# A four-layer mixer trunk on one core: first weights ahead of the second modulation blocks, products after each chunk pair, two-pass gate products, a shorter reciprocal root, and another order in the last pair's halves

## The chip, the core and the metric

The kernel runs on one core of a Trainium2 chip. TensorE (PE) multiplies matrices, VectorE (DVE), ScalarE (ACT) and GpSimd (POOL) work on elements, SyncE (SP) and the queues of the other engines issue transfers. The metric is the time of one execution in device microseconds; lower is better. The figure that counts is the median of the runs of a kernel.

## The reference, cut to what matters

The trunk runs 512 latent tokens and 256 context tokens of width 1024 through four layers. Layer i uses mixer i % 3: a gated linear attention in chunks (GLA, layers 0 and 3), a windowed attention (layer 1), a recurrent unit (RG-LRU, layer 2). Each mixer is wrapped in norms with a modulation (shift, scale, gate) that comes from a conditioning vector. Only the latent tokens are returned.

```
def rmsnorm(x, g):
    xf = x.astype(jnp.float32)
    y = xf * lax.rsqrt(jnp.mean(xf * xf, axis=-1, keepdims=True) + EPS)
    return (y * g.astype(jnp.float32)).astype(x.dtype)
...
    def project(h):
        q, k, v, z = jnp.split(h @ w_in, [GLA_DK, 2 * GLA_DK, 2 * GLA_DK + GLA_DV], axis=-1)
        la_f, la_b = [split_heads(jax.nn.log_sigmoid(((h @ w_g1[d]) @ w_g2[d] + b_g[d]).astype(jnp.float32)) / GLA_TAU, GLA_HEADS)
                      for d in range(2)]
```

The change touches the gates' two small products (h @ w_g1 of rank 16 for each of two directions, then @ w_g2), the norms, and the order in which the first layer starts.

## The kernel before

**Tiling.** The width of 1024 is KC = 8 chunks of 128 rows. Activations lie transposed, 128 channels x 768 tokens for each chunk (256 context tokens, then 512 latent ones). Every operand of a large product is split in two terms of reduced precision, a high part and a remainder: `Rh` and `Rl` for activations, `wh` and `wl` for weights. One product is then three matmuls for each chunk (Rh with wh, Rl with wh, Rh with wl). Weights arrive as fp32 in a buffer `raw` (or `rawp` in the start); ScalarE casts the high part (L266) and VectorE, or GpSimd for every third, subtracts the remainder (L269).

**Stages.** `first_norm` reads x, normalises it, transposes it into `OG` and modulates it; then come the four mixers (`gla`, attention, LRU, `gla`), each followed by `finish`: out-projection (L796), post-norm, residual, and the next layer's norm and transposes (L638). A mixer's engines are ordered by a scheduler that goes by priorities. Two places have their order written out for TensorE, ScalarE and VectorE with `tc.manual_schedule`: the loop over n in `first_norm`, and the middle of `finish`.

**The start.** The modulation of layer 0 comes in eight blocks m of one MB. `mod_part` fetches a block (L511) and multiplies it with the conditioning vector (L524, into 32 partitions); `mod_ss` copies the result (L537), transposes it (L542) and adds it up to the scale and shift of two chunks (L543, L549, L555). Blocks n and n + 4 together give the modulation of chunks 2n and 2n + 1. `modulate` (L703, L704, L708) then makes Rh and Rl of a chunk. Round n of the loop takes blocks n and n + 4 and modulates two chunks. `products` (L728) are matmuls of the layer's first products, chunk by chunk as Rh and Rl appear: `todo[:2]` is the gates' first weight w1 (128 columns, of which each group of 32 holds the two directions' 16), `todo[2:]` the first head's q and k (`wqk`: k for the context, k and q for the latent tokens). The fetches are issued in the order x, blocks 0 and 4, w1 (`load_g1`), wqk, blocks 1 and 5, 2 and 6, 3 and 7, save that each `fetch` stands where the code puts it: the first one (w1) before blocks 1 and 5, the second (wqk) before blocks 3 and 7.

**The first head.** `gates` multiplies t1 (what w1 gave) with the second weight g2 (L979), applies log-sigmoid on ScalarE (L983 to L996) and builds running sums on VectorE (L989, L993). `levels` makes factors X and Y for each level of the chunked recurrence (L1049, L1110), copies Y to K (L1096) and multiplies them in small matmuls of 32 columns (L1062). `values` (L1034) are the head's v products. `spread` deals the side work (values) out between the levels, by a total in ns.

**The norms.** `rstd_of` turns a sum of squares into a reciprocal root with two GpSimd instructions: times 1/n plus EPS (L614), then a power of -0.5 (L615). It serves the norm of x (tile `rx`, 24 of them), the post-norm (`ry`, 22, after a reduction of two half sums in `post`, L810), and the gate-head norm (`ro`, 20).

**finish.** `halves(...)` runs the second 512 output columns for pairs of (half of the depth, tile of 128 tokens). After the second half of a tile it takes the square sums (L803) and the gate multiply (L804), and `post` makes the reciprocal root. `residual` (L816), `square` (L621) and `scale` (L823) follow, then the transposes of the pair.

## Time and profile before

| what | value |
|---|---|
| median of 3 runs | 1518.22 us (1516.42 to 1520.79) |
| profiled execution, its own time | 1513.64 us |
| its span in the profile | 1511.8 us |
| TensorE busy | 1442.0 us, 95% |
| VectorE, ScalarE, GpSimd busy | 67%, 52%, 13% |
| chain that ended last, by engine | PE 54%, DVE 10%, ACT 5%, DMA 4% |

The profiled execution is one run, and its time lies under the median of the three; durations of instructions are read from it. Stages in us from the span's start: start 0 to 62, layer 0 to 370, its finish to 455, layer 1 to 790, its finish to 880, layer 2 to 1115, its finish to 1226, layer 3 to 1460, its finish to the end. In a timeline row the first number is the start, the second the time that the named instructions took, and the bracket holds the idle time before them and what ended it.

### The profile page before, as it was taken

The page shows a single profiled execution, that of the slowest core. Times are in us where ns is not written, and L with a number is a line of the kernel's source. Part 1 is how long each engine was busy: PE and PEld are TensorE (multiplying, and loading weights), DVE is VectorE, ACT ScalarE, POOL GpSimd, SP SyncE. Part 2 cuts the span into 40 slices and gives each one's busy share as a digit, 9 for nine tenths or more (in the row PEclk, how much of TensorE's full clock was granted, in tenths as well). Part 3 has the DMA queues.
Part 4 walks back from the last instruction along what each step waited for, and adds up shares of the span by engine and source line. Part 5 has one row for each costly group of instructions (what it writes and reads, how often), then busy time and mean ns, then how long its engine had stood idle before and what let it go on. Part 6 is the DMA issues. An engine that isn't in the chain of part 4 may idle for free.

```text
span 1511.8 us, 29077 instructions
## 1 busy us (share of the span) xinstructions
PE 1442.0 (95%) x11691; PEld 1206.4 (80%) x11691; DVE 1010.5 (67%) x1914; ACT 784.2 (52%) x1541; POOL 189.4 (13%) x300
## 2 busy tenths in 40 slices
PE   5988999999999899999999999899999999999998
PEld 3877888888877778878888787788878778889886
DVE  5576657576264389787883568988972667676854
ACT  5535353624252367656662477878842555364441
POOL 2202100112022200010000210000011211101111
PEclk8999999999999999999999999999999999999999
DMA  9441514112574542122216625212252342121232
GB/s 300 145 147 53 169 38 135 57 34 76 203 237 140 174 112 68 31 65 57 57 56 224 217 79 152 82 50 71 67 177 64 103 145 91 46 60 57 60 111 85
DMA packets 153046, 162.35 MB, mean 107 GB/s; under 512 B 12418, under 2 KB 141968, under 8 KB 152912
## 3 DMA queue, kind: packets, MB, share of 16 engines
q1 hardware_dynamic: 147456, 146.56, 31.4%
q10 hardware_dynamic: 5456, 13.94, 2.6%
q8 instruction: 92, 1.51, 0.4%
q14 instruction: 42, 0.34, 0.1%
HBM read 138.44 MB, written 11.53 MB: 99 GB/s over the span
## 4 chain that ended last, share of the span: by engine, by line
PE 54%; DVE 10%; ACT 5%; DMA 4%; issue 2%; SPq 1%; POOL 1%; ACTq 0%; DVEq 0%; POOLq 0%
PE mxt L796 14%; PE pjt L395 9%; PE pjt L385 9%; PE pjt L1034 4%; PE mxt L1532 3%; PE mxt L1516 2%; PE sct L1637 2%; PE mxt L524 1%; PE mxt L1475 1%; PE mxt L1194 1%; DVE wl L269 1%; PE mxt L1458 1%; DMA bb<-in_b_mod_dram 1%; DMA raw<-in_w_mod_dram 1%; PE sct L1062 1%
## 5 line engine op out<-in xcount | busy, mean ns | idle before, releaser
L385 PE MATMUL pjt<-Rh,wh 128*128 128x256 f32 (+1 forms) x592 | 199.0, 337 | 5.3 <-DVE Rh L649 3.3
L385 PE MATMUL pjt<-Rl,wh 128*128 128x256 f32 (+1 forms) x592 | 198.2, 336 | 2.0 <-DVE Rl L650 1.6
L385 PE MATMUL pjt<-Rh,wl 128*128 128x256 f32 (+1 forms) x592 | 197.1, 334 | 0.7 <-DVE wl L269 0.7
L269 DVE TENSOR_TENSOR wl<-raw,wh 128x1024 fp32r<-128x1024 f32 x106 | 129.7, 1237 | 51.2 <-ACT wh L266 50.6
L395 PE MATMUL pjt<-Rh,wl 128*128 128x512 f32 (+1 forms) x448 | 160.3, 358 | 0.0
L395 PE MATMUL pjt<-Rl,wh 128*128 128x512 f32 (+1 forms) x448 | 159.8, 357 | 0.0
L395 PE MATMUL pjt<-Rh,wh 128*128 128x512 f32 (+1 forms) x448 | 159.5, 356 | 0.0
L266 ACT CAST wh<-raw 128x1024 fp32r<-128x1024 f32 x118 | 121.4, 1051 | 71.6 <-PE mxt L796 33.0
L796 PE MATMUL mxt<-wh,Rh 128*128 128x512 f32 x352 | 138.9, 395 | 0.0
L796 PE MATMUL mxt<-wh,Rl 128*128 128x512 f32 x352 | 137.6, 391 | 0.8 <-DVE Rl L769 0.8
L796 PE MATMUL mxt<-wl,Rh 128*128 128x512 f32 x352 | 137.2, 390 | 0.0
L385 PEld LDWEIGHTS pjt<-Rh,wh 128*128 128x128 f32 x592 | 112.5, 191 | 17.0 <-DVE Rh L649 4.4
L385 PEld LDWEIGHTS pjt<-Rl,wh 128*128 128x128 f32 x592 | 112.6, 190 | 14.6 <-DVE Rl L650 3.8
L385 PEld LDWEIGHTS pjt<-Rh,wl 128*128 128x128 f32 x592 | 112.6, 191 | 12.6 <-DVE wl L269 1.2
L1034 PE MATMUL pjt<-wl,Rh 128*128 128x256 f32 x384 | 110.6, 288 | 0.0
L1034 PE MATMUL pjt<-wh,Rh 128*128 128x256 f32 x384 | 109.8, 286 | 0.0
L1034 PE MATMUL pjt<-wh,Rl 128*128 128x256 f32 x384 | 109.5, 285 | 0.0
L1494 ACT ACTIVATE pe<-mxt,mxs 128x256 f32<-128x256 f32 (+2 forms) x128 | 70.7, 556 | 52.6 <-DVE mxs L1486 51.9
L395 PEld LDWEIGHTS pjt<-Rh,wl 128*128 128x128 f32 x448 | 84.6, 189 | 9.8 <-issue 1.9
L395 PEld LDWEIGHTS pjt<-Rh,wh 128*128 128x128 f32 x448 | 84.7, 189 | 9.2 <-issue 1.2
L395 PEld LDWEIGHTS pjt<-Rl,wh 128*128 128x128 f32 x448 | 84.7, 189 | 9.2 <-issue 1.3
L804 DVE TENSOR_TENSOR y<-mxt,gpt 128x512 f32<-128x512 f32 x44 | 30.3, 689 | 73.9 <-ACT y L803 73.8
(295 smaller groups left out, 3480.9 us busy)
## 6 DMA issues: line engine op xcount, KB each, us to landing
rawp<-in_w_mod_dram SPq DMA_DIRECT2D x48, 512.0 KB, 5.8
raw<-in_w_mod_dram SPq DMA_DIRECT2D x48, 512.0 KB, 4.4
raw<-in_a_w_in_dram SPq DMA_DIRECT2D x32, 512.0 KB, 3.5
raw<-in_b_w_in_dram SPq DMA_DIRECT2D x20, 512.0 KB, 4.9
raw<-in_c_w_in_dram SPq DMA_DIRECT2D x20, 512.0 KB, 3.6
xd<-x SPq DMA_DIRECT2D x18, 512.0 KB
raw<-in_a_w_out_dram SPq DMA_DIRECT2D x16, 512.0 KB, 3.5
x<-xd ACTq DMA_DIRECT2D x16, 512.0 KB, 8.9
```

The source lines that it names most:

```text
L266: S.copy(h, x)
L269: e.tensor_tensor(l, x, h.bitcast(F32), op=ALU.subtract)
L385: PE.matmul(ps, w[u][:, k, c0 : c0 + P], R[v][:, k, t0 : t0 + n], start=(k == 0 and u + v == 0), stop=(k == KC - 1 and u == 1),)
L395: PE.matmul(ps, w[u][:, k, c0 : c0 + P], R[x][:, k, t0 : t0 + n], start=(k == 0 and u + x == 0), stop=(k == KC - 1 and u == 1),)
L524: PE.matmul(ps[32 * g : 32 * g + 32, 0:256], sT[:, k, :], r2[k // 4][:, k % 4, :], start=(n < 4), stop=(n >= 4), skip_group_check=True,)
L796: PE.matmul(ps, l[:, tt * P : (tt + 1) * P], r, start=(k == 0 and u + v == 0), stop=(k == kc - 1 and u == 1),)
L804: V.tensor_tensor(y[tt][:, c], ps, gpt[:, 1 if tt >= 4 else 0, c], op=ALU.mult)
L1034: PE.matmul(ps[:, n, :], R[u][:, k, tt * P : (tt + 1) * P], w[x][:, k, :], start=(k == 0 and u + x == 0), stop=(k == KC - 1 and u == 1),)
L1494: S.activation(p[:, o : o + w], u[e][:, :w], AF.Exp, bias=nm, scale=0.125, accum_out=den[:, n : n + 1],)
L1516: PE.transpose(u[e][:, c * P : (c + 1) * P], ps[e][:, m * P : (m + 1) * P], ident)
L1532: PE.matmul(po[64 * e : 64 * e + 64, 0:P], v[:, keys[m], 64 * kv : 64 * kv + 64], pt[:, e, m * P : (m + 1) * P], start=(m == len(keys) - 1 ...
L1637: PE.matmul(ps[:, t0 : t0 + nn], wg[a][:, n, :], x[c][:, p0 : p0 + nn], start=(q == 0), stop=(q == 2),)
```

## The change

Six things change.

1. **Gate weights in two passes.** `load_g1` packs w1 in one tile: column groups 0 to 2 hold the high part, group 3 the remainder. A product with w1 is then two matmuls for each chunk instead of three, and the second weight g2 is loaded into all four groups of 32 rows, so that L979 uses 128 rows instead of 96. The conversion is three casts and one subtraction instead of four and four; a load of g2 issues two DMAs more (six before, eight now, half of them on ScalarE's queue and half on SyncE's).
2. **Order of fetches in the start.** w1 and wqk are fetched after blocks 0 and 4, ahead of all others; wqk's casts and subtractions stand in round 0's modulation.
3. **Order of products in the start.** Round n now reads: blocks n and n + 4, qk products of chunk 2n - 2, transposes, modulation of chunks 2n and 2n + 1, qk products of chunk 2n - 1, w1 products of chunks 2n and 2n + 1. The qk products of chunks 6 and 7 follow the loop.
4. **Reciprocal root.** The mean's factor goes into the Square activation; EPS is added on VectorE (for `rx` and `ro`) or in the addition of the two half sums (`ry`). GpSimd keeps the power alone.
5. **Last pair of a finish.** The halves run tile by tile, (0,2), (1,2), (0,3), (1,3), and tile 2's residual, square and scale come earlier.
6. **First head.** The total by which values are dealt to the levels is 24 * 6 * GDV / 2.4 instead of 24 * 4 * GDV / 2.4 where no head comes before.

```diff
@@ load_g1
         def convert():
-            w1h = wp.tile([P, KC, 256], F32R, name="wh", tag="wh")
-            w1l = wp.tile([P, KC, 256], F32R, name="wl", tag="wl")
-            for g in range(4):
-                c = slice(32 * g, 32 * g + 32)
-                S.copy(w1h[:, :, c], rv)
-                V.tensor_tensor(w1l[:, :, c], rv, w1h[:, :, c].bitcast(F32), op=ALU.subtract)
-            return w1h, w1l
+            w1 = wp.tile([P, KC, 256], F32R, name="wh", tag="wh")
+            S.copy(w1[:, :, 0:32], rv)
+            V.tensor_tensor(w1[:, :, 96:128], rv, w1[:, :, 0:32].bitcast(F32), op=ALU.subtract)
+            for g in range(1, 3):
+                S.copy(w1[:, :, 32 * g : 32 * g + 32], w1[:, :, 0:32].bitcast(F32))
+            return (w1,)
...
@@ load_g2
-                for g in range(3):
+                for g in range(4):
...
@@ ws_part, and the same in products
+    def terms(w):
+        return ((0, 0), (0, 1), (1, 0)) if len(w) > 1 else ((0, 0), (0, 1))
...
-            for u, v in ((0, 0), (0, 1), (1, 0)):
+            for u, v in terms(w):
...
@@ rstd_of
-    def rstd_of(pool, ss, n, name):
+    def rstd_of(pool, ss, name, eps=True):
         w = ss.shape[1]
         r = pool.tile([P, w], F32, name=name, tag=name, bufs=4)
-        G.tensor_scalar(r, ss, 1.0 / n, EPS, op0=ALU.mult, op1=ALU.add)
-        G.tensor_tensor(r, r, nhalf.to_broadcast([P, w]), op=ALU.pow)
+        if eps:
+            V.tensor_scalar(r, ss, EPS, None, op0=ALU.add)
+        G.tensor_tensor(r, r if eps else ss, nhalf.to_broadcast([P, w]), op=ALU.pow)
         return r
...
@@ first_norm
         for n in range(4):
-            if n in (1, 3):
-                fetch()
-                convert()
             for m in (n, n + 4):
                 f = mod_ss(i, m, bank, sp, 10)
                 next(f)
                 parts.append(f)
+            if n == 0:
+                for _ in range(2):
+                    fetch()
+                    convert()
...
                 next(a)
-                if n == 2:
-                    products(todo[:2], range(0, 2))
-                if n == 3:
-                    products(todo[2:], range(0, 3))
                 next(b)
-                if n == 3:
-                    products(todo[:2], range(4, 6))
+                if n:
+                    products(todo[2:], (2 * n - 2,))
                 run(a)
                 run(b)
-                if n == 2:
-                    products(todo[:2], range(2, 4))
-                if n == 3:
-                    products(todo[2:], range(3, 6))
                 modulate(2 * n)
                 modulate(2 * n + 1)
-        products(todo[:2], range(6, 8))
-        products(todo[2:], range(6, 8))
+                if n:
+                    products(todo[2:], (2 * n - 1,))
+                products(todo[:2], (2 * n, 2 * n + 1))
+        products(todo[2:], (KC - 2, KC - 1))
...
@@ finish
-                S.activation(y[tt][:, c], ps, AF.Square, accum_out=ssq[tt][:, ch : ch + 1])
+                S.activation(y[tt][:, c], ps, AF.Square, scale=D ** -0.5, accum_out=ssq[tt][:, ch : ch + 1])
...
-                V.tensor_reduce(s1, ssq[tt], axis=AX.X, op=ALU.add)
-                rs[tt] = rstd_of(fp, s1, D, "ry")
+                V.scalar_tensor_tensor(s1, ssq[tt][:, 0:1], EPS, ssq[tt][:, 1:2], op0=ALU.add, op1=ALU.add)
+                rs[tt] = rstd_of(fp, s1, "ry", False)
...
-                h = halves((0, 2), (0, 3), (1, 2), (1, 3))
+                h = halves((0, 2), (1, 2), (0, 3), (1, 3))
...
                 step((0, 1), 0)
+                residual(2)
                 next(h)
                 norm((0, 1), 1)
+                square(2)
                 run(h)
-                residual(2)
                 norm((0, 1), 2)
-                square(2)
+                scale(2)
+                norm((0, 1), 3)
                 residual(3)
-                norm((0, 1), 3)
-                scale(2)
                 square(3)
                 scale(3)
...
@@ gla
-                            ps[:, t0 : t0 + n], g2[:96, d, h * P : (h + 1) * P], t1[:96, t0 : t0 + n],
+                            ps[:, t0 : t0 + n], g2[:, d, h * P : (h + 1) * P], t1[:, t0 : t0 + n],
...
-                nz = nz if prev else 0
-                spread(lv, side, len(LEVELS), 24 * (nz + 4 * GDV) / 2.4)
+                spread(lv, side, len(LEVELS), 24 * (nz + 4 * GDV if prev else 6 * GDV) / 2.4)
```

In the order after, line numbers are those of the changed file (L524 is L528, L728 is L735, L542 is L546, L703 is L710, L1110 is L1112). TensorE in the start, before: after round 0's transposes the blocks of rounds 1 and 2 follow, with products between them only from round 2 on.

```order
L524 MATMUL mxt<-rawp,sT 32x256 x8
L542 MATMUL pjt<-ident,mp 128x128 x2
L542 MATMUL mxt<-ident,mp 128x128 x2
L524 MATMUL pjt<-rawp,sT 32x256 x8
L524 MATMUL mxt<-rawp,sT 32x256 x8
L542 MATMUL pjt<-ident,mp 128x128 x2
L542 MATMUL mxt<-ident,mp 128x128 x2
L524 MATMUL pjt<-rawp,sT 32x256 x8
L728 MATMUL sct<-Rh,wh 128x256
```

The same place after; the last rows are the qk products of chunk 0, three to a group.

```order
L735 MATMUL sct<-Rh,wh 128x512
L735 MATMUL sct<-Rl,wh 128x512
L735 MATMUL sct<-Rh,wh 128x512
L735 MATMUL sct<-Rl,wh 128x512
L528 MATMUL pjt<-rawp,sT 32x256 x8
L528 MATMUL mxt<-rawp,sT 32x256 x8
L735 MATMUL sct<-Rh,wh 128x256
L735 MATMUL sct<-Rl,wh 128x256
L735 MATMUL sct<-Rh,wl 128x256
```

The blocks of round 1 now stand behind the w1 products of chunks 0 and 1 (the first four rows), which read Rh and Rl of this round.

ScalarE in the start, before: copies of blocks 0 and 4 (L537) around the casts of w1 (L286), then both chunks' Rh (L703), then the next blocks.

```order
L537 COPY mp<-pjt 128x256
L683 COPY OGb<-mxt 128x2x256
L286 CAST wh<-rawp 128x8x32 x4
L537 COPY mp<-mxt 128x256
L703 ACTIVATE Rh<-OG,modT 128x256
L703 ACTIVATE Rh<-OG,modT 128x512
L703 ACTIVATE Rh<-OG,modT 128x256
L703 ACTIVATE Rh<-OG,modT 128x512
L537 COPY mp<-pjt 128x256
```

After:

```order
L541 COPY mp<-mxt 128x256
L266 CAST wh<-rawp 128x1024
L710 ACTIVATE Rh<-OG,modT 128x256
L266 CAST wh<-rawp 128x1024
L710 ACTIVATE Rh<-OG,modT 128x512
L710 ACTIVATE Rh<-OG,modT 128x256
L710 ACTIVATE Rh<-OG,modT 128x512
L541 COPY mp<-pjt 128x256
L541 COPY mp<-mxt 128x256
```

The two casts of wqk (L266) came in round 2 before and now stand between the pieces of round 0's first chunk.

VectorE in the first head of layer 0, before (L269 are remainders of the next weights, L574 and L576 belong to the gate modulation, L1042 to the values).

```order
L269 TENSOR_TENSOR wl<-raw,wh 128x1024
L574 TENSOR_TENSOR gb<-mxt,gb 128x256
L998 COPY tl<-ls 128x12
L1110 TENSOR_TENSOR X<-X,tmp 128x384x2
L269 TENSOR_TENSOR wl<-raw,wh 128x1024
L576 TENSOR_TENSOR ml<-gb,mh 128x256
L1042 TENSOR_TENSOR OGb<-pjt,v 128x512
L1110 TENSOR_TENSOR Y<-Y,tmp 128x384x2
L1110 TENSOR_TENSOR Y<-Y,ls 128x192x2x2
```

After:

```order
L1112 TENSOR_TENSOR X<-X,tmp 128x384x2
L1112 TENSOR_TENSOR Y<-Y,tmp 128x384x2
L1044 TENSOR_TENSOR OGb<-pjt,v 128x512
L1000 COPY tl<-ls 128x12
L578 TENSOR_TENSOR gb<-mxt,gb 128x256
L269 TENSOR_TENSOR wl<-raw,wh 128x1024
L580 TENSOR_TENSOR ml<-gb,mh 128x256
L269 TENSOR_TENSOR wl<-raw,wh 128x1024
L1112 TENSOR_TENSOR X<-X,ls 128x192x2x2
```

X and Y of the first of these levels now follow one another, and both remainders of the next weights stand behind them. On ScalarE in the same head the three activations of the LRU parameters (L177 to L179) have moved behind the gates' exponential, with two more table loads.

## Rows read from the trace of the kernel before

**Rows 1.** Stages: length, busy time of PE, PEld, DVE, ACT, POOL, granted clock, DMA, GB/s

```profile
0.00:62.00 62.00, 45.79 (x313) 32.82 (x314) 32.43 (x70) 30.66 (x55) 18.18 (x30) 0.92 0.77 236
455.00:790.00 335.00, 320.17 (x2529) 266.98 (x2529) 244.53 (x730) 187.46 (x562) 35.99 (x24) 1.00 0.29 83
1226.00:1460.00 234.00, 231.63 (x2398) 199.94 (x2397) 166.10 (x266) 114.80 (x198) 28.72 (x59) 1.00 0.23 69
```

**Rows 2.** The same columns for short stretches around a low clock

```profile
22.00:26.00 4.00, 1.73 (x20) 0.62 (x18) 3.17 (x12) 2.63 (x7) 0.79 (x1) 1.00 1.06 354
26.00:36.20 10.20, 7.00 (x44) 3.84 (x45) 6.50 (x15) 4.39 (x9) 2.67 (x3) 0.50 1.11 323
1203.60:1210.40 6.80, 5.77 (x27) 5.58 (x27) 4.06 (x8) 4.14 (x10) 0.38 (x1) 0.50 0.07 17
```

**Rows 3.** Timeline of TensorE in the start: start, us, what, [idle before]

```profile
24.17 1.07 PE L524 MATMUL pjt<-rawp,sT 128*32 128x256 f32 x16 [0.67 <-DMA rawp<-in_w_mod_dram]
28.07 1.94 PE L524 MATMUL mxt<-rawp,sT 128*32 128x256 f32 x16 [2.83 <-DMA rawp<-in_w_mod_dram]
...
32.36 1.93 PE L524 MATMUL pjt<-rawp,sT 128*32 128x256 f32 x16 [1.12 <-DMA rawp<-in_w_mod_dram]
...
48.03 1.07 PE L524 MATMUL mxt<-rawp,sT 128*32 128x256 f32 x16
...
51.24 0.38 PE L542 MATMUL pjt<-ident,mp 128*128 128x128 f32 x2
...
65.29 0.87 PE L979 MATMUL sct<-t,g 96*128 96x256 f32 x4
```

**Rows 4.** Timeline of ScalarE (first row) and VectorE in the start

```profile
38.86 1.05 ACT L266 CAST wh<-rawp 128x1024 fp32r<-128x1024 f32 x1
...
27.30 1.02 DVE L708 TENSOR_TENSOR Rl<-xn,Rh 128x512 fp32r<-128x512 f32 x1
...
55.52 1.05 DVE L708 TENSOR_TENSOR Rl<-xn,Rh 128x512 fp32r<-128x512 f32 x1
```

**Rows 5.** Timeline of the first head in layer 0: ScalarE, VectorE, TensorE

```profile
69.24 1.28 ACT L988 ACT_TABLE_LOAD   x1
...
82.72 1.23 DVE L269 TENSOR_TENSOR wl<-raw,wh 128x1024 fp32r<-128x1024 f32 x1 [2.33 <-ACT wh L266]
...
85.00 1.64 DVE L1110 TENSOR_TENSOR X<-X,tmp 128x768 f32<-128x768 f32 x1
...
88.52 1.65 DVE L1110 TENSOR_TENSOR Y<-Y,tmp 128x768 f32<-128x768 f32 x1
...
90.80 1.11 PE L1062 MATMUL sct<-X,K 128*32 128x32 f32 x48 [3.44 <-ACT K L1096]
```

**Rows 6.** Timeline at the end of layer 0's finish

```profile
453.61 2.59 POOL L269 TENSOR_TENSOR wl<-raw,wh 128x1024 fp32r<-128x1024 f32 x1
...
453.88 3.41 DVE L816 SCALAR_TENSOR_TENSOR x<-y,ry,x 128x1024 f32<-128x1024 f32 x1
...
457.68 0.51 PE L385 MATMUL pjt<-Rh,wh 128*128 128x256 f32 x2 [1.96 <-DVE Rh L649]
```

**Rows 7.** Timeline at the end of layer 2's finish

```profile
1202.72 0.63 POOL L614 TENSOR_SCALAR rx<-ssx 128x1 f32<-128x1 f32 x1 [0.40 <-ACT y L621]
...
1204.02 0.75 DVE L823 TENSOR_SCALAR y<-x,rx 128x1024 f32<-128x1024 f32 x1 [0.72 <-POOL rx L615]
...
1204.83 3.46 PE L638 MATMUL mxt<-ident,y 128*128 128x128 f32 x15 [1.03 <-DVE y L823]
```

**Rows 8.** Chain that ended last, a head of layer 3: start, us, what

```profile
1258.76 2.88 PE pjt L385 x24
...
1261.86 5.48 PE pjt L385 x24
```

**Rows 9.** Timeline of VectorE and GpSimd in the last tile's norm

```profile
1506.11 0.14 DVE L810 TENSOR_REDUCE s<-ssq 128x1 f32<-128x2 f32 x1
1506.35 0.19 POOL L614 TENSOR_SCALAR ry<-s 128x1 f32<-128x1 f32 x1 [4.61 <-DVE s L810]
1506.62 0.55 POOL L615 TENSOR_TENSOR ry<-ry,nhalf 128x1 f32<-128x1 f32 x1
```

More of the change, by code (lines that the diff above doesn't have):

```diff
@@ L383, in ws_part @@
         for k in range(KC):
-            for u, v in ((0, 0), (0, 1), (1, 0)):
+            for u, v in terms(w):
                 PE.matmul(
                     ps, w[u][:, k, c0 : c0 + P], R[v][:, k, t0 : t0 + n],
-                    start=(k == 0 and u + v == 0), stop=(k == KC - 1 and u == 1),
+                    start=(k == 0 and u + v == 0), stop=(k == KC - 1 and (u, v) == terms(w)[-1]),
                 )
@@ L620, in unit_rstd @@
         ss = pool.tile([P, 1], F32, name="ssx", tag="ssx", bufs=4)
-        S.activation(xn, x, AF.Square, accum_out=ss)
-        return rstd_of(pool, ss, D, "rx")
+        S.activation(xn, x, AF.Square, scale=D ** -0.5, accum_out=ss)
+        return rstd_of(pool, ss, "rx")
     def unit(pool, x, xn):
@@ L726, in products @@
                 for k in ks:
-                    for u, v in ((0, 0), (0, 1), (1, 0)):
+                    for u, v in terms(w):
                         PE.matmul(
@@ L730, in products @@
                             start=(k == 0 and u + v == 0 and not (w is wqk and stream == "ctx")),
-                            stop=(k == KC - 1 and u == 1), skip_group_check=True,
+                            stop=(k == KC - 1 and (u, v) == terms(w)[-1]), skip_group_check=True,
                         )
@@ L955, in gla @@
             g2 = mp.tile([P, 2, 512], F32R, name="g2")
-            S.copy(g2[:96], g2r[:96])
+            S.copy(g2, g2r)
             G.tensor_tensor(g2[32:64], g2r[32:64], g2[32:64].bitcast(F32), op=ALU.subtract)
@@ L1195, in chunk @@
                     for n in range(2):
-                        S.activation(on[:, n, :], ps[:, n, :], AF.Square, accum_out=ss[:, n : n + 1])
+                        S.activation(on[:, n, :], ps[:, n, :], AF.Square, scale=GDV ** -0.5, accum_out=ss[:, n : n + 1])
                     V.tensor_tensor(on, ps, gh.unsqueeze(1).to_broadcast([P, 2, GDV]), op=ALU.mult)
-                    rs = rstd_of(mp, ss, GDV, "ro")
+                    rs = rstd_of(mp, ss, "ro")
                     for n in range(2):
```

## Prediction, made before the changed kernel ran

> **What bounds the kernel now.** I read the stage windows first, then the timelines at the places the change touches, then the chain of waits. In the windows TensorE is busy for 231.63 of 234 us in layer 3, but only 45.79 of 62 us in the start [rows 1]. So a product that goes away is worth its own duration where TensorE is full, and nothing where TensorE waits for something else. The chain prices a product at 2.88/24 = 0.12 us for 256 columns and 5.48/24 = 0.228 us for 512 [rows 8].
>
> In the start the bound is first the landing of the modulation blocks: TensorE waits 0.67, 2.83 and 1.12 us for three of them in a row [rows 3]. A block m (one MB) lands about every 3.9 us: 24.17, 28.07, 32.36 [rows 3]. Then TensorE has products queued ahead of each block, and the blocks at 48.03 and the transposes at 51.24 follow without a wait; the gates' matmuls (L979) start at 65.29 [rows 3].
>
> The granted clock is 0.50 from 26 to 36.2 us, after a stretch in which TensorE was busy 1.73 of 4 us, and 0.50 again at 1203.6 [rows 2]; that is the 1.2 GHz level, and a block's matmuls then take 1.94 us in place of 1.07 [rows 3].
>
> The profiled execution took 1513.64 us, 1.84 outside its span, and lies 4.58 under the median of 1518.22. I make the sum against it and put the difference on the median.
>
> **Start: cost +3.5 us (0 to +7).** The new order of fetches puts the first-head weights (qk0) in the slot where m1 landed, and every later block one slot on: qk0 at about 24.2, m1 28.1, m5 32.3 (the three landing times above, shifted by one). After that the order on TensorE decides. Each round n now reads: two blocks, one chunk's qk products, transposes, one more chunk's qk products, the gate-weight products of this round's two chunks; and the next round's blocks stand behind those gate-weight products, which wait for this round's modulation. Before, the products of one round were queued over the blocks of the next, and nothing waited for the newest modulation. So the rounds become a serial chain, and I price one: two blocks 2 x 1.07 = 2.1; one chunk of qk products 3 x (0.12 + 2 x 0.228) = 1.72, which covers the copy of the block to SBUF; from the transposes (51.24) to the end of the last residual (55.52 + 1.05 = 56.57) 5.33 us [rows 3, 4]; the last gate-weight product 0.3. That is 9.4 us for a round in which TensorE has about 7.4 us of work (2.1 + 2 x 1.72 + 0.4 of transposes + 4 x (0.12 + 0.228)).
>
> Round 0 ends later than its 28.32 (27.30 + 1.02 [rows 4]), because the casts and subtractions of qk0 now stand between its modulations: two casts of 1.05 on ScalarE, two subtractions of 1.23 on VectorE [rows 4, 5], some 2.4 us, so 30.7. Round 1 is then held by m5 at 32.3, not by round 0: 32.3 + 1.07 + 1.72 + 5.33 + 0.3 = 40.7. Rounds 2 and 3 follow at 50.2 and 59.6; m7 is the last block in both orders, was used at 48.03 without a wait [rows 3], and is not awaited here either. Behind them come the qk products of the last two chunks, 2 x 1.72, and the 24 of q for the context, 2.88: L979 at 65.9 instead of 65.29, so +0.6 at full clock. The packed gate weights save 8 x (0.12 + 0.228) = 2.8 us of products here, but they sit in a chain that waits, so I cost their gain at nothing; it would count only if TensorE were full.
>
> The clock comes on top. Round 1 starts after waits like the one that halved it before; at 0.50 its block costs 0.87 more and its qk products 1.72 more, so +2.8; a later round at half costs 3.6 (two blocks 1.8, products 1.7). I take one round at half: 0.6 + 2.8 = +3.5. No round at half is the lower end, about 0; two are the upper, +7. There is hardly a gain below nothing, since the chain begins at a landing which the diff does not advance.
>
> **First head of layer 0: -3 us (-5 to -1).** TensorE waits 3.44 us at 90.80 for the first level's factors; VectorE made X at 85.00 and Y only at 88.52, because conversions of the next weights stood ahead of them, one after a wait of 2.33 us for the cast [rows 5]. In the new order X and Y of that level stand together ahead of these conversions. That brings Y forward by about 5 us against the gates. Against it, the LRU parameters on ScalarE have slipped behind the gates' exponential, which adds two table loads of 1.28 us [rows 5], some 1.3 of which falls on the chain. The dealt values (the total of the spread is raised by a half, 10240 to 15360 ns) then fill more of TensorE's waits between the levels; I count that within the same range. The lost time of 3.44 us plus the half clock that follows it is what can be won.
>
> **The mean's scaling and EPS.** The reciprocal root loses its first GpSimd instruction, 66 times over the program. Most lie beside a full TensorE. Where the norm is the end of the chain, the price is 0.19 to 0.63 us [rows 7, 9]; for 44 of the 66 VectorE gets an addition instead, near the 0.14 us of the reduction in the tail [rows 9]. Layer 0's finish: TensorE waits 1.96 us, behind a residual that took 3.41 us beside a GpSimd subtraction of 2.59 [rows 6]. The halves of the last pair now go by tiles, so the first tile's residual comes earlier and only one is left at the end: -1 (-2 to -0.4). Layer 1's finish, where I found hardly a wait: -0.2. Layer 2's finish: the last transposes wait for the scaling at 1204.02, behind two reciprocal roots [rows 7], so -0.9; of layer 3's 24 gate-weight products saved (24 x 0.12 = 2.88 us [rows 8]) 16 fall into that same wait and only 8 lie behind it, 0.96, or 1.9 at the clock of 0.50 there [rows 2]. Together -2 (-2.8 to -0.7). The 20 gate-head norms: -0.5 (-1 to +0.5), mostly under a full TensorE. The final tail loses 1506.35 to 1506.62: -0.3 [rows 9].
>
> **The sum.** +3.5 - 3 - 1 - 0.2 - 2 - 0.5 - 0.3 = -3.5: the profiled execution would be 1510.1, the median **1514.7**. All best ends: 0 - 5 - 2 - 0.2 - 2.8 - 1 - 0.3 = -11.3, 1506.9; all worst: 7 - 1 - 0.4 - 0 - 0.7 + 0.5 - 0.2 = +5.2, 1523.4.
>
> **Rivals.** *Faster: the start costs nothing.* The clock rises with round 1 and stays, and the first head wins its whole wait: 0.6 - 5 - 4 = -8.4, so 1509.8. For it speaks that the wait of 1.96 us at 457.68 did not lower the clock (1.00 over the stage [rows 1, 6]), and a round's idle time is 9.4 - 7.4 = 2.0 us. Against it: the serial rounds leave no slack for anything late.
>
> *Slower: every round begins cold.* The rounds' short products and 2 us waits keep the clock at 0.50 through rounds 1, 2 and 3: 0.6 + 2.8 + 3.6 + 3.6 = +10.6; the first head wins only 1, since its table loads eat the rest, and the finishes 4: +5.6, 1523.8. The wait of 2.83 us, after which the clock was 0.50 [rows 2, 3], speaks for it; the wait of 1.96 against. It decides from three cold rounds on; two leave the kernel within the measurement. The Trainium skill, "TensorE: Matmul & The Clock Gate", section "HAM oscillation", states this pattern: short products per K-tile, with a longer wait for the next slice, let the clock be throttled again in each tile. By that rule this rival's time holds; the row at 457.68 does not bear it out for a wait of this size.
>
> *No change at all.* Start and head cancel exactly and the norms lie under TensorE: 1517 to 1518, inside the forecast's class.
>
> **Chances.** 0.3% (4.55 us) is about what a measurement of this kernel can tell from no change: faster is below 1513.67, slower above 1522.77. The forecast and the third case (within) 0.50, the first rival and the near half of the forecast's error on that side 0.38, the cold rounds 0.12. The range goes to 1506.5 and 1523: each end lets out about one in ten.
>
> **What would show it.** In the changed trace: the first qk0 cast at about 24.2 us, the second chunk's residual at about 30.7; rounds ending near 41, 50 and 60 with one wait of about 2 us each before the gate-weight products; the clock row of 30 to 45 us at 0.50 for one round only; L979 between 66 and 72. TensorE's wait before the first level's large batch should shrink from 3.44 to under 1.5 us. The wait after layer 0's finish should fall below 1.5 us. If L979 comes before 63, the serial chain is wrong; if the first level still waits for Y behind a conversion, the second term is.

## The result, and the profile after

The changed kernel took **1542.05 us** in the median of 4 runs (1536.47 to 1544.84), the kernel before 1518.65 on the same chip: a ratio of 1.0149 with a 95% interval of 1.0122 to 1.0176. It is 23.4 us slower; the forecast was 1514.7 with a range to 1523. The profiled execution took 1541.82 us with a span of 1540.0.

Each run lists its span and its mean granted clock. Span times clock is a rough time at the full clock, what is left is the clock's share: 1497.6 and 18.4 us before (mean of 75 runs), 1516.1 and 23.5 us after (4 runs). So some 5 us of the loss are clock, and 18.5 are not; runs of one kernel scatter by several us in the clock's share, so the split is rough.

Where do they arise? I compared the start of each TensorE instruction that has the same place in both traces. The changed kernel is 4.9 us late when the values of the first head begin (67 us of before), 6.3 at 115, 8.7 at 165, 12.4 at 200, 15.2 at the end of layer 0, 19.4 at 520, 20.5 at 860, 22.5 at 890, 23.4 at 1245 and 28.7 at 1500. The start accounts for a sixth; the rest arises everywhere. Attention and LRU are not touched by the diff but for the norms that feed them, and they lose too. Not all of that need be the change: the trace of before is one quick run, and gates_ry (below), whose time is that of before, loses 4.9 us against it between 470 and 790, where the changed kernel loses 3.5.

The list of waits says on what. First after, then before: engine, line, what is waited for: us in total, times, longest.

```profile
PE mxt L528 <- DMA raw<-in_w_mod_dram: 11.7, 11, 2.5
...
PE sct L735 <- POOL Rl L715: 6.5, 7, 1.4
PE mxt L1209 <- DVE on L1202: 6.2, 11, 0.9
...
PE mxt L644 <- DVE y L824: 5.1, 4, 2.8
PE mxt L1157 <- ACT st L1179: 4.6, 1, 4.6
```

```profile
PE mxt L524 <- DMA raw<-in_w_mod_dram: 8.3, 9, 1.5
...
PE mxt L638 <- DVE y L823: 1.8, 2, 1.0
...
PE mxt L1166 <- ACT st L1177: 1.6, 1, 1.6
...
PE mxt L1207 <- DVE on L1200: 1.3, 4, 0.5
```

Five waits grew: in the start for GpSimd's part of this round's Rl (L735), of which the list of before has none; for the scaled gate head (L1209); for the scaled row of a finish (L644); for the state after the first head's levels (L1157 here, L1166 before); and for modulation weights that arrive when TensorE reaches them (L528). The first four come and go with edits in the runs below. The fifth does not: the 8.3 us of before are the least of all 20 traces, and gates_ry has 10.4.

**The start** lost about what was forecast, though not step by step. TensorE after, blocks of rounds 1, 2, 3 and the first gates' matmul (columns as in [rows 3]):

```profile
33.27 1.94 PE L528 MATMUL pjt<-rawp,sT 128*32 128x256 f32 x16
...
45.44 1.57 PE L528 MATMUL pjt<-rawp,sT 128*32 128x256 f32 x16
...
55.70 1.07 PE L528 MATMUL pjt<-rawp,sT 128*32 128x256 f32 x16
...
70.21 0.28 PE L981 MATMUL sct<-t,g 128*128 128x256 f32 x1
```

A round takes 12.2 us where the clock is low in part of it and 10.3 then, a serial chain somewhat longer than worked out (9.4), and L981 begins at 70.21 where L979 began at 65.29 [rows 3]. Over the ten traces with the new order of products this moment lies between 67.2 and 72.2 us, over the nine with the old one between 63.7 and 67.2. Five-microsecond windows show the clock: 0.60 at 25, 0.50 at 30, 0.87 at 35, and again 0.81 and 0.85 from 40 to 50. Before, they read 0.60, 0.50 and 0.88, and then 1.00. The third line is before's (columns as in [rows 1]):

```profile
25.00:30.00 5.00, 1.55 (x3) 0.76 (x3) 4.36 (x7) 3.30 (x5) 1.47 (x1) 0.60 1.08 355
...
40.00:45.00 5.00, 3.28 (x12) 2.22 (x10) 2.88 (x6) 2.23 (x4) 1.75 (x2) 0.81 1.10 318
...
40.00:45.00 5.00, 4.90 (x39) 3.58 (x38) 4.38 (x7) 3.71 (x6) 1.59 (x1) 1.00 1.04 325
```

**The first head.** VectorE, ScalarE and TensorE after, where the first level's Y becomes K:

```profile
89.15 1.73 DVE L1112 TENSOR_TENSOR Y<-Y,tmp 128x768 f32<-128x768 f32 x1
...
92.79 1.04 ACT L266 CAST wh<-raw 128x1024 fp32r<-128x1024 f32 x1 [1.85 <-DMA raw<-in_a_w_in_dram]
...
94.76 1.06 ACT L1098 COPY K<-Y 128x384 f32<-128x384 f32 x2
...
95.39 1.14 PE L1064 MATMUL sct<-X,K 128*32 128x32 f32 x48 [3.26 <-ACT K L1098]
```

ScalarE at the same place before:

```profile
90.20 1.00 ACT L1096 COPY K<-Y 128x384 f32<-128x384 f32 x2 [4.19 <-DVE Y L1110]
```

Y ends at 90.88, hardly later than before (90.17 [rows 5]) though the gates are 6 us later. But K, which followed Y at once before, is copied 3.9 us after it: two casts of the next weights stand ahead of it on ScalarE, the second behind a wait of 1.85 us for its transfer.

TensorE, GpSimd and ScalarE after, around the state that follows the levels:

```profile
128.21 0.52 PE L1157 MATMUL mxt<-ident,Y 128*128 128x128 f32 x2 [4.61 <-ACT st L1179]
...
123.27 3.80 POOL L1140 TENSOR_TENSOR A<-A,dg 32x96 f32<-32x96 f32 x4
...
127.52 0.64 ACT L1179 COPY st<-mxt 128x256 f32<-128x256 f32 x2
```

The same place before:

```profile
120.16 0.39 PE L1166 MATMUL mxt<-v,kth 128*128 128x256 f32 x1 [1.63 <-ACT st L1177]
...
116.34 2.68 POOL L1138 TENSOR_TENSOR A<-A,dg 32x96 f32<-32x96 f32 x4
```

The state's copy (L1179) stands on ScalarE behind a cast that waits for GpSimd's four additions; they take 3.80 us instead of 2.68. TensorE waits 4.61 us in one piece, where before it waited 0.83, 1.21, 1.63 and 0.93, together as much, and then it runs at half clock (0.53):

```profile
128.20:131.80 3.60, 3.59 (x14) 3.10 (x15) 2.17 (x4) 3.32 (x4) 0.49 (x1) 0.53 0.43 136
```

**The gate-head norm.** After, then before: the end of the second square sum on ScalarE, the gate multiply, the reciprocal root and the scaling.

```profile
149.79 0.20 ACT L1198 ACTIVATION_READ_ACCUMULATOR on<-mxt 128x1 f32 x1
...
150.83 0.68 DVE L1199 TENSOR_TENSOR on<-mxt,gh 128x512 f32<-128x512 f32 x1
151.43 0.16 DVE L620 TENSOR_SCALAR ro<-sso 128x2 f32<-128x2 f32 x1
152.40 0.61 DVE L1202 TENSOR_SCALAR on<-on,ro 128x256 f32<-128x256 f32 x2 [0.80 <-POOL ro L621]
...
151.67 0.69 POOL L621 TENSOR_TENSOR ro<-ro,nhalf 128x2 f32<-128x2 f32 x1 [4.89 <-DVE ro L620]
```

```profile
141.15 0.20 ACT L1196 ACTIVATION_READ_ACCUMULATOR on<-mxt 128x1 f32 x1
...
142.19 0.68 DVE L1197 TENSOR_TENSOR on<-mxt,gh 128x512 f32<-128x512 f32 x1
143.13 0.35 DVE L1200 TENSOR_SCALAR on<-on,ro 128x256 f32<-128x256 f32 x1 [0.26 <-POOL ro L615]
...
141.44 0.89 POOL L614 TENSOR_SCALAR ro<-sso 128x2 f32<-128x2 f32 x1 [3.81 <-ACT on L1196]
142.41 0.69 POOL L615 TENSOR_TENSOR ro<-ro,nhalf 128x2 f32<-128x2 f32 x1
```

Before, GpSimd worked while VectorE still multiplied; the scaling started 1.78 us after the sum (143.13 - 141.35). After, the addition (L620, 0.16 us long) stands in VectorE's queue behind X (L1051) and the gate multiply, which don't concern it; GpSimd gets its input at 151.67, and the scaling starts 2.41 us after the sum. Over the 20 such norms the median of this distance went from 1.37 to 2.34 us, the total from 29.4 to 45.0.

### The profile page after: what moved, and what is told of

Its sections match the earlier page's. It is cut to its first block, busy times and chain, and to the rows that moved or that the text cites. A ratio compares the mean times of both kernels' runs of the same rounds, so it can differ in the third digit from the quotient of the medians.

```text
span 1540.0 us, 28940 instructions
## 1 busy us (share of the span) xinstructions
PE 1449.9 (94%) x11651; PEld 1209.6 (79%) x11651; DVE 1014.7 (66%) x1952; ACT 785.7 (51%) x1541; POOL 167.9 (11%) x234
## 4 chain that ended last, share of the span: by engine, by line
PE 47%; DVE 11%; ACT 7%; DMA 5%; issue 3%; POOL 1%; SPq 1%; DVEq 0%; ACTq 0%; POOLq 0%
PE mxt L797 14%; PE pjt L399 8%; PE pjt L389 8%; PE pjt L1036 4%; PE mxt L1533 3%; PE mxt L1517 2%; DMA raw<-in_w_mod_dram 2%; PE sct L1638 2%; PE mxt L528 2%; PE mxt L1476 1%; DVE wl L269 1%; ACT wh L266 1%; PE mxt L1459 1%; PE sct L1064 1%; DVE Rl L656 1%
## 5 line engine op out<-in xcount | busy, mean ns | idle before, releaser
L389 PE MATMUL pjt<-Rh,wl 128*128 128x256 f32 (+1 forms) x568 | 190.7, 337 | 0.8 <-DVE wl L269 0.8
L269 DVE TENSOR_TENSOR wl<-raw,wh 128x1024 fp32r<-128x1024 f32 x106 | 130.2, 1241 | 50.6 <-ACT wh L266 50.1
L266 ACT CAST wh<-raw 128x1024 fp32r<-128x1024 f32 x118 | 121.2, 1050 | 70.4 <-PE mxt L797 33.4
L389 PEld LDWEIGHTS pjt<-Rh,wl 128*128 128x128 f32 x568 | 108.1, 191 | 12.7 <-DVE wl L269 1.2
L399 PEld LDWEIGHTS pjt<-Rh,wl 128*128 128x128 f32 x448 | 85.1, 190 | 9.8 <-issue 2.0
```

Source lines behind the costliest of these rows:

```text
L266: S.copy(h, x)
L269: e.tensor_tensor(l, x, h.bitcast(F32), op=ALU.subtract)
L389: PE.matmul(ps, w[u][:, k, c0 : c0 + P], R[v][:, k, t0 : t0 + n], start=(k == 0 and u + v == 0), stop=(k == KC - 1 and (u, v) == terms(w)[ ...
L399: PE.matmul(ps, w[u][:, k, c0 : c0 + P], R[x][:, k, t0 : t0 + n], start=(k == 0 and u + x == 0), stop=(k == KC - 1 and u == 1),)
```

## The experiments

Each run was timed beside the kernel before, whose medians lay between 1517.1 and 1518.8 us on the chips used; a difference between two runs is uncertain by about a microsecond for that alone. "Changed" is the changed kernel, 1542.05 us. A hunk "taken back" is the diff above, reversed.

**1. What each edit gives back.** Five runs each take one edit out of the changed kernel.

```diff
 # undo_start: first_norm, fetches and products in the old order
-            if n == 0:
-                for _ in range(2):
+            if n in (1, 3):
...
 # undo_rstd: the old reciprocal root in all norms
-        if eps:
-            V.tensor_scalar(r, ss, EPS, None, op0=ALU.add)
+        G.tensor_scalar(r, ss, 1.0 / n, EPS, op0=ALU.mult, op1=ALU.add)
...
 # undo_spread
-  24 * (nz + 4 * GDV if prev else 6 * GDV) / 2.4
+  24 * ((nz if prev else 0) + 4 * GDV) / 2.4
...
 # undo_gates: three passes for w1, groups of g2 and conversion as before
 # undo_halves
-                h = halves((0, 2), (1, 2), (0, 3), (1, 3))
+                h = halves((0, 2), (0, 3), (1, 2), (1, 3))
```

> The changed kernel with the start's order of fetches and of products put back, all else as changed. In the traces the changed kernel is 4.6 to 6.3 us late when the gates' matmuls begin, and 28 us at the end. Theory A (each part costs by itself; the VectorE additions of the reciprocal root carry the most): the start gives back its own 5 us, so about 1537 us. Rival B (a late start shifts everything behind it into other waits and cold clocks): nearly all comes back, 1515 to 1522 us.

Measured 1528.37 us, ratio to before 1.0065 (1.0042 to 1.0089): 13.7 us come back, between theory A and B.

> The changed kernel with the old reciprocal root: GpSimd scales and adds EPS, VectorE has no addition in that chain. Theory A: VectorE, which works in order, stood behind each addition until the square sum was there; TensorE's waits for the gate-head norm (6.2 us against 1.3) and for the scaled row of the finishes (5.1 against 1.8) go back, with one or two half-clock spells of 1.7 us: 8 to 12 us faster than the changed kernel, 1530 to 1534 us. Rival B: it saves nothing, or costs 2 us, since the removed GpSimd instruction comes back: 1541 to 1544 us.

Measured 1532.49, 1.0093 (1.0062 to 1.0124): 9.6 us, theory A.

> The changed kernel with the old total for dealing the first head's values. The changed kernel waits 4.61 us at 128.2 for the state behind GpSimd's additions, where before three waits of together 3.67 us stood; a half-clock spell of 1.7 us follows. Theory A: with a third of the values left over after the levels this wait is filled: 2 to 4 us faster than the changed kernel, 1538 to 1540 us. Rival: the values are lacking between the levels instead, and the time stays within 2 us of 1542.

Measured 1534.12, 1.0108 (1.0077 to 1.0139): 7.9 us, more than either expected. The wait of 4.61 us is gone from this trace (1.48 and 2.41 us stand there).

> The changed kernel with three passes for the gates' first product, and the conversion in four groups. If the two passes are worth what TensorE saves where it is full, this is 1 to 4 us slower than the changed kernel: 1543 to 1546 us. Rival: the changed order of conversions and the two added transfers cost more than the passes save, and this is 2 to 5 us faster: 1537 to 1540 us.

Measured 1540.51, 1.0143 (1.0107 to 1.0178): between the two ranges, no difference that could be told. The wait of 4.61 us is gone here too (1.36): it takes more than the dealing to make it, and without it the time is no better.

> The changed kernel with the last pair's halves in the old order. Beside two-pass gates alone the new order cost 4.2 us (1520.98 against 1516.78). Theory A (the parts' prices add up): 1536 to 1539 us. Rival B (in the changed kernel the finishes' end is covered or hidden by other losses): 1541 to 1543 us.

Measured 1538.06, 1.0134 (1.0109 to 1.0159): 4.0 us less than the changed kernel, theory A, though the intervals overlap.

The five sum to 36.7 us (35.2 without the gates), more than the 23.4 that are there: they are not independent.

**2. What each edit costs alone,** on the kernel before. The edit is the hunk of the diff that the name says.

> The kernel before with the start's two new orders alone. Theory A (the start costs what its undoing gave back, whatever else is changed): 12 to 15 us slower than before, 1530 to 1533 us. Rival B (half of it comes from the meeting with the other changes): 5 to 8 us slower, 1523 to 1526 us.

Measured 1520.45, 1.0025 (1.0015 to 1.0036). Rival B, even less: +2.8 us. In its trace TensorE is 5.2 us late at the first head and 5.4 us late at the end, so nothing is lost or won after it. (Both against the trace of before, a quick run; so more than the 2.8.)

> The kernel before with the new reciprocal root alone, in all three norms. In the changed kernel the time from the end of the second square sum of the gate-head norm to the start of its scaling has a median of 2.34 us, before 1.37, summed over 20 norms 45.0 against 29.4. Theory A (the addition on VectorE is one hop more, and stands behind other VectorE work): 6 to 10 us slower than before, 1524 to 1528 us, and the same 2.3 us. Rival B (it hurts only where the dealt values and the late start leave TensorE without cover): within 3 us of before.

Measured 1523.87, 1.0046 (1.0028 to 1.0064): +6.2 us, theory A. The chain's median is 2.40 us here too. Its trace loses 3.8 us from 118 to 375 and 3.7 from 1300 to 1500, in the two GLA layers where the gate-head norm is, and about 1 us in between. Layer 3 shows it in all traces: between 1300 and 1458 the eight with the addition on VectorE lose 3.6 to 3.8 us, the other eleven -0.1 to 0.3.

> The kernel before with the two-pass gates, the new order of the last pair's halves, and the shorter reciprocal root of the post-norm alone, where EPS goes into the addition of the two half sums and no VectorE addition comes in; start, dealing and the other norms as before. Theory A (these three only take work away): 2 to 6 us faster than before, 1512 to 1516 us. Rival B: the moved instructions of the scheduler and of the finish give it back: 1516 to 1520 us.

Measured 1520.98, 1.0020 (1.0007 to 1.0032): slower, where theory A had it faster, and slightly above rival B's range. Its trace is 3.0 us early at 165; then come a wait for modulation weights with a low clock at 174 (2.7 us) and, at the ends of the finishes, 1.9 us in layer 0 and 2.0 in layer 1. The second of these, here and before:

```profile
875.37 1.06 ACT L626 ACTIVATE y<-x 128x1024 f32<-128x1024 f32 x1 [0.89 <-DVE x L821]
...
876.42 0.58 ACT L808 ACTIVATE y<-mxt 128x512 f32<-128x512 f32 x1
...
881.85 1.28 DVE L821 SCALAR_TENSOR_TENSOR x<-y,ry,x 128x1024 f32<-128x1024 f32 x1
885.25 0.75 DVE L828 TENSOR_SCALAR y<-x,rx 128x1024 f32<-128x1024 f32 x1 [2.13 <-POOL rx L620]
...
886.07 0.55 PE L643 MATMUL mxt<-ident,y 128*128 128x128 f32 x3 [1.27 <-DVE y L828]
```

```profile
870.00 0.60 ACT L803 ACTIVATE y<-mxt 128x512 f32<-128x512 f32 x1
...
875.14 1.28 DVE L816 SCALAR_TENSOR_TENSOR x<-y,ry,x 128x1024 f32<-128x1024 f32 x1
...
878.86 0.75 DVE L823 TENSOR_SCALAR y<-x,rx 128x1024 f32<-128x1024 f32 x1 [0.71 <-POOL rx L615]
```

The second half of the last tile is taken (L808) at 876.42 instead of 870.00, because on ScalarE the square of tile 2 (L626, 875.37) stands ahead of it and waits for tile 2's residual. This stretch lies 4.4 us later in general; the last residual is 6.7 us later (881.85 to 875.14) and the last scaling 6.4, and TensorE waits for it. From 860 to 890 the ten traces with the new halves lose 1.9 to 2.3 us, the nine with the old ones -0.1 to 0.2; at layer 0's finish the two groups overlap.

> The kernel before with the two-pass gates and the shorter reciprocal root of the post-norm alone; halves in the old order. With the new halves it was 1520.98 us, and in its trace about 2 us went at the end of each of the finishes of layers 0 and 1, where the square sum of the last tile stands behind the square of tile 2 on ScalarE. Theory A (the order of the halves costs this, and more behind it): 1513 to 1516 us. Rival B (the halves are neutral, and the loss is the two passes' new order of conversions): 1519 to 1522 us.

Measured 1516.78, 0.9999 (0.9988 to 1.0009): the time of before, nearer to theory A than to B. The difference to the run above, 4.2 us by the medians and 3.2 by the ratios, whose intervals just touch, is the order of the halves. Span times clock is 1495.0, 2.6 us under before, which fits the products saved in the two passes; the shorter post-norm is in this run too.

**3. Two repairs of order.**

```diff
 # gates_ry_halves_mended
                 norm((0, 1), 1)
-                square(2)
                 run(h)
+                square(2)
                 norm((0, 1), 2)
                 scale(2)
-                norm((0, 1), 3)
                 residual(3)
+                norm((0, 1), 3)
```

> As gates_ry, with the new order of the halves by tiles, but with the square of tile 2 put behind the last tile's square sum on ScalarE. Theory A (only that place on ScalarE costs; tile by tile is otherwise as good or better): within 2 us of gates_ry, and the last scaling of layer 1's finish comes no later than before. Rival B (tile by tile is worse in itself): as with the new halves, about 1521 us.

Measured 1523.32, 1.0034 (1.0019 to 1.0050): no gain, rival B. In its trace ScalarE takes the last tile in time, and the last residual and scaling come 2.1 and 2.5 us later than before in a stretch that is 2.4 us late, so this place is mended. But 2.3 us go just behind it: on VectorE a subtraction for the next weights (L269, at 880.01 before) now stands ahead of the remainder that TensorE needs (L655).

```profile
877.25 1.28 DVE L821 SCALAR_TENSOR_TENSOR x<-y,ry,x 128x1024 f32<-128x1024 f32 x1
...
881.32 0.75 DVE L828 TENSOR_SCALAR y<-x,rx 128x1024 f32<-128x1024 f32 x1 [0.72 <-POOL rx L620]
...
886.36 1.22 DVE L269 TENSOR_TENSOR wl<-raw,wh 128x1024 fp32r<-128x1024 f32 x1
887.49 0.69 DVE L655 TENSOR_TENSOR Rl<-y,Rh 128x512 fp32r<-128x512 f32 x1
...
888.23 0.39 PE L389 MATMUL pjt<-Rl,wh 128*128 128x256 f32 x1 [1.35 <-DVE Rl L655]
```

This trace (1517.89 us) is one of the two quickest of seven runs, so it does not show all that the median loses.

In the start, the old order of products with the new order of fetches, and the new fetches with products one round later:

```diff
 # gates_ry_start_mended
                 next(a)
                 next(b)
                 if n:
-                    products(todo[2:], (2 * n - 2,))
+                    products(todo[:2], (2 * n - 2, 2 * n - 1))
                 run(a)
                 run(b)
                 modulate(2 * n)
                 modulate(2 * n + 1)
                 if n:
-                    products(todo[2:], (2 * n - 1,))
-                products(todo[:2], (2 * n, 2 * n + 1))
+                    products(todo[2:], (2 * n - 2, 2 * n - 1))
+        products(todo[:2], (KC - 2, KC - 1))
         products(todo[2:], (KC - 2, KC - 1))
```

> The changed kernel with the old order of products in the start, and the new order of fetches kept. Putting back both gave 1528.4 us against 1542.1. Theory A (the products that make the next blocks wait for this round's modulation carry the cost): 1527 to 1533 us. Rival B (the weights ahead of the blocks, with their casts inside the first modulation, carry it): 1538 to 1543 us.

Measured 1528.80, 1.0072 (1.0056 to 1.0088), theory A, as with both put back: the order of products carries the start's cost, the order of fetches is free.

> As gates_ry, with the start's new order of fetches, and the products one round later: blocks of round n, then the gate-weight products of round n-1, transposes, then both qk products of round n-1 while round n is modulated. So the next blocks do not wait for this round's modulation. Theory A (the wait of the blocks for the modulation is the start's whole cost): a round is 7.4 us of TensorE work instead of a chain of 9.4, the gates' matmuls begin at 60 to 63 us, and the kernel is 1 to 4 us faster than gates_ry. Rival B (the clock, at half after the first landings, or a landing holds the rounds): they begin at 65 to 68 us, and the time is that of gates_ry or up to 3 us more.

Measured 1518.06, 1.0005 (0.9988 to 1.0021): rival B. First this kernel, then gates_ry:

```profile
29.80 1.94 PE L528 MATMUL pjt<-rawp,sT 128*32 128x256 f32 x16 [7.18 <-DMA rawp<-in_w_mod_dram]
...
65.57 0.86 PE L980 MATMUL sct<-t,g 128*128 128x256 f32 x4
```

```profile
41.90 1.07 PE L528 MATMUL pjt<-rawp,sT 128*32 128x256 f32 x16 [3.06 <-DMA rawp<-in_w_mod_dram]
...
65.69 0.87 PE L985 MATMUL sct<-t,g 128*128 128x256 f32 x4
```

Without the serial rounds L980 is back at 65.6, but no earlier: with the weights fetched first TensorE waits 7.18 us for the next block. The saved 2.8 us of products do not show in either.

**4. Which edits meet.**

> The kernel before with the start's new orders and the new total for dealing the first head's values, nothing else. The start alone cost 2.8 us (1520.45), undoing it in the changed kernel gave back 13.7, undoing the dealing 7.9. Theory A (the two meet in the first head: values are dealt out where a late start leaves no cover, and the wait for the state at the end of the levels grows, with a cold clock behind it): 6 to 10 us slower than before, 1524 to 1528 us. Rival B (they add up simply; the dealing alone does nothing or gains): 1519 to 1522 us.

Measured 1523.88, 1.0045 (1.0028 to 1.0061). It lies at the lower edge of theory A, but the place that A names is wrong: its trace is 4.3 us late at 67 and 4.9 at 375, and loses 3.9 us between 1245 and 1300, in layer 3's first head, where no start is near. That head has no head before it either, so its values are dealt by the same total. The nine traces with the new total lose 1.3 to 3.9 us there, the ten with the old one nothing (-0.03 to 0.02); TensorE waits there for the remainder of a transposed Y, 2.38 us in this run and 1.60 in the changed kernel, whose row is:

```profile
1293.95 0.44 PE L1157 MATMUL mxt<-ident,Y 128*128 128x128 f32 x2 [1.60 <-DVE ktl L1161]
```

So dealing costs about 3.4 us beside the start, by the difference to only_start; no run has it alone, and a meeting of the two does not show.

> The kernel before with the start's new orders and the new reciprocal root. Alone they cost 2.8 and 6.2 us; the start put back in the changed kernel gave 13.7. Theory A (these two meet: late gates and a later norm leave TensorE's waits long enough for a cold clock in layer 0): 12 to 17 us slower than before, 1529 to 1534 us. Rival B (their sum): 7 to 11 us, 1524 to 1528 us.

Measured 1534.47, 1.0112 (1.0082 to 1.0142): +16.4 us where the parts give 2.8 + 6.2 = 9.0, theory A. Span times clock is 1512.5, against 1497.6 + 4.0 + 5.2 = 1506.8 from the parts alone; the four runs scatter from 1508.7 to 1517.5, so the meeting is likely rather than sure. In its trace layer 0 loses 5.5 us between 118 and 375, 1.7 more than with the reciprocal root alone.

**5. The reciprocal root.**

```diff
 # undo_ro: the changed kernel, EPS of the gate-head norms on GpSimd
-            V.tensor_scalar(r, ss, EPS, None, op0=ALU.add)
+            (G if name == "ro" else V).tensor_scalar(r, ss, EPS, None, op0=ALU.add)
...
 # gates_no_eps: two passes, and the power alone
+        G.tensor_tensor(r, ss, nhalf.to_broadcast([P, w]), op=ALU.pow)
...
 # gates_eps_act (on before, with two passes), changed_eps_act (changed kernel)
+            S.activation(r, ss, AF.Identity, bias=epst)
```

> The changed kernel with EPS of the 20 gate-head norms added on GpSimd again; the other norms keep the VectorE addition. All of the new reciprocal root put back gave 9.6 us. Theory A (the hop to VectorE in the gate-head norms is the cost): 1532 to 1536 us, and the median from square sum to scaling back near 1.4 us. Rival B (the norms of the finishes carry it): 1539 to 1542 us.

Measured 1533.46, 1.0114 (1.0091 to 1.0138): theory A, 8.6 of the 9.6 us come from the 20 gate-head norms; the median is 1.37 us again.

> The kernel before with two-pass gates and all norms with one GpSimd power and no EPS at all (EPS is left out of the pre-norms and gate-head norms), so neither the old GpSimd scaling nor the new VectorE addition is there. Theory A (the chain to the reciprocal root is worth what its steps take: shorter by about 0.3 to 0.5 us in each gate-head norm): 3 to 7 us faster than before, 1510 to 1514 us. Rival B (a shorter chain gains nothing, only a longer one loses): 1515 to 1518 us, like gates_ry.

Measured 1513.15, 0.9970 (0.9951 to 0.9990): theory A. The chain's total is 27.2 us; without any third step the edit is worth 0.3%, some 4 us, beside gates_ry (0.9999; the intervals just touch). It leaves EPS out, so it is no kernel to keep.

> The kernel before with two-pass gates and the shorter reciprocal root, but EPS is added on ScalarE, right behind the square sum that ScalarE itself makes, so that no further engine comes into the chain (square sum and EPS on ScalarE, power on GpSimd, scaling on VectorE). Without EPS at all it was 4.9 us faster than before. Theory A (it was the hop to a third engine that cost, and one GpSimd instruction less is worth 0.2 to 0.5 us in each chain): the median from square sum to scaling 1.3 us or less, and 1512 to 1516 us, faster than both kernels. Rival B (ScalarE is held by other work there as VectorE was): above 1518 us.

Measured 1522.20, 1.0028 (1.0015 to 1.0041): rival B, slower than before. The norm on ScalarE and GpSimd:

```profile
139.90 0.38 ACT L495 ACTIVATE gz<-pjt 128x256 f32<-128x256 f32 x1
140.16 0.30 ACT L622 ACTIVATE ro<-sso,epst 128x2 f32<-128x2 f32 x1
...
140.54 0.93 POOL L623 TENSOR_TENSOR ro<-ro,nhalf 128x2 f32<-128x2 f32 x1 [4.27 <-ACT ro L622]
```

Even on the engine that made the sum, the addition is put behind another activation (L495). The median is 1.64 us, the total 32.5, over the 29.4 of two GpSimd instructions.

> The changed kernel whole, with EPS on ScalarE instead of VectorE, nothing else. Theory A (the hop to VectorE is the price of the reciprocal root): as with the old reciprocal root put back, 1530 to 1534 us, or up to 3 us less. Rival B: 1538 to 1543 us.

Measured 1541.66, 1.0145 (1.0126 to 1.0164): rival B. The chain's total falls from 45.0 to 32.6 us and the time does not. So the length of this chain alone does not explain the 8.6 us of undo_ro. Its trace tells where: layer 3 loses only 0.2 us between 1300 and 1458 (changed: 3.6), as if the addition had never gone to VectorE, but 5.9 us go between 890 and 1245, in layer 2 and its finish (changed: 0.9), and 6.7 between 67 and 165 (changed: 3.8). The run also puts the EPS of the 24 norms of x on ScalarE, and every such edit gives the scheduler another order; which of the two costs this is left open. Span times clock fell from 1516.1 to 1512.4, the clock's share rose from 23.5 to 27.3 us.

No version with EPS beat the kernel before; gates_ry equals it.

## Why the prediction was wrong, by its steps

- **Start, +3.5 (0 to +7): right in size, in part by luck.** Alone +2.8 us, and L981 at 70.2 lies in 66 to 72. The serial chain was right, but the rounds ended at 45.4, 55.7 and 65.4 us and not near 41, 50 and 60. Round 1 was not held by the landing of m5: its two blocks stand behind round 0's gate-weight products, which, with their waits for ScalarE's and GpSimd's parts of the modulation, last until 33.27. And I added 2.8 for a round at half clock, though before has its own low clock there: by the windows it cost some 6.8 us after and 5.1 before, 1.7 more. Only the blocks of round 1 ran at half, its qk products did not; the end of round 1 and part of a block of round 2 did. Too little for the chain and too much for the clock cancelled.
- **First head, -3 (-5 to -1): wrong size and given back.** X and Y did come forward: the gates end 6.0 us late, Y only 0.7. But I followed VectorE and not ScalarE: K's copy slipped behind two casts there, so the first level's batch is 4.6 us late, and TensorE still waits 3.26 us instead of the 1.5 I named. Then comes the one wait of 4.61 us at the state, and half clock. I counted the dealing "within the same range"; it costs 3.4 us beside the start alone and 7.9 in the changed kernel, part of it in layer 3's first head, which I did not price at all.
- **Gate-head norms, -0.5 (-1 to +0.5): the step that failed most.** With the other norms it measured +6.2 alone, and 8.6 by itself in the changed kernel. I priced the addition by its own 0.14 us [rows 9] and did not ask what is queued ahead of it on VectorE. Two GpSimd instructions were one hop; VectorE and GpSimd in turn are two, behind other work. TensorE was not full enough to cover it: its wait for the scaled gate head went from 1.3 to 6.2 us. That the longer chain is all of the cost is not shown (changed_eps_act).
- **The finishes of layers 0, 1 and 2, -1, -0.2 and -2: wrong sign in the first two.** The changed trace loses 2.0 us at the end of each of these, and TensorE waits 1.79 us after layer 0's (472.9), not under the 1.5 I named; from 1110 to 1245, at layer 2's, it gains 0.4. With the old halves (undo_halves) it loses nothing at the first two and gains 2.0 at the third: that term was right but for the halves, which cost about 4 us in all. I followed the first tile, which does come earlier, and not the last one, whose square sum stands behind the first tile's square. That a queue is in order was in front of me, since the order is written out by hand there.
- **Two passes:** right in the start, where they gave nothing; span times clock shows 2.6 us for them with the post-norm, and the timed runs nothing (gates_ry).
- **The rivals.** The slower one named the clock alone, in the start alone. The clock's share did rise by 5 us, but over layers 0 and 1 and the end of layer 2 (4.61 us of wait at 128.2, then 0.53), not in three cold rounds; of this, layer 1's part stands in the trace of gates_ry too. The Trainium skill, "TensorE: Matmul & The Clock Gate", section "HAM oscillation", describes bursts that start cold after each wait, with waits longer than the bursts. By my own sum a round had 7.4 us of work and 2.0 of waiting, so the section did not speak for this rival as I had it; here the blocks of round 1, the end of that round and part of a block of round 2 ran cold, the later rounds not.

Alone the parts sum to 2.8 + 6.2 + 4.2 + 3.4 - 0.3 = 16.3 us (start, reciprocal root, halves, dealing, gates_ry). (The shorter post-norm is in two of these.) Some 7 us remain for their meeting; start_rstd shows such a meeting, of 7.4 us by medians, but not by what mechanism.

## What to carry to other kernels

An instruction that moves to another engine costs what stands ahead of it in that engine's queue and one more hand-over, not its own duration: 0.16 us of addition made a chain 1 us longer, 20 times. The same holds for what a forecast moves forward: Y came 5 us earlier against the gates, and its copy waited on the next engine. In an order written by hand, follow the last tile's chain through each queue, and look at each instruction that waits with a ready one behind it. Where a kernel is 95% full on one engine, edits on the others have little to win, and a new wait can also cost the clock (4.61 us at 128.2, then 0.53).

## What the runs showed of the hardware

The same kernel's clock share scatters from 13.6 to 25.8 us over 75 runs of before, with times from 1513.5 to 1523.4; a single trace of it (1513.64 us, 4.6 under the median of its kernel) is a lucky one, and differences of traces overstate what a change costs (28.2 against 23.4 us here). Four small GpSimd additions (L1140) took 1.70 to 1.88 us in 14 of 16 places of the two traces, 2.68 where they ran 1.1 us beside a VectorE subtraction of the next weights, and 3.80 where they ran 2.5 us beside two. Waits of about 2 us went either way with the clock: after 1.79 us at 472.9 (after) TensorE ran at 0.54, after 1.96 us at 457.68 (before) at 1.00.
